# A hybrid encoder block on one Trainium2 core: two input groups without GpSimd, half of the shift made by narrow fp32 products

## The chip, the core and the metric

The kernel runs on one core of one Trainium2 chip, in one launch. The metric is the device time of that launch in microseconds (us). A core has TensorE (PE, matrix products into PSUM), VectorE (DVE), ScalarE (ACT), GpSimd (POOL), and SyncE (SP), which issues most of the loads here.

## What is computed

The reference is one layer of an encoder block with batch 1, 512 positions and 2048 channels, in fp32. Only its beginning is touched:

```python
mod = jax.nn.silu(c) @ w_ada + b_ada                 # c: (1, 2048), w_ada: (2048, 6*2048)
shift1, scale1, gate1, shift2, scale2, gate2 = jnp.split(mod, 6, axis=-1)
h = rms_norm(x, norm1_w) * (1 + scale1) + shift1
p = h @ w_in                                         # Fourier | q | k | v | o gate | i/f gates
...
x = x + gate1 * (mix @ w_out)                        # mix: Fourier and mLSTM heads
h2 = rms_norm(x, norm2_w) * (1 + scale2) + shift2
...
return rms_norm(x, norm_f_w)
```

The normalisation factor of a position (one over the root mean square of its 2048 channels) is known only when all of x has been read, and a channel of scale1 or shift1 only when 2048 weights have been multiplied with silu(c) and summed.

## The kernel before, in words

x lies transposed: sixteen tiles of 128 channels by 512 positions. An fp32 product is made of three products of a reduced type (F32R), high part by high, high by remainder, remainder by high: `kouter` (L231 to L237) issues these three for every PSUM bank of a group, for one channel tile k (a step). `split` (L113 to L122) makes the high part of a weight tile on ScalarE (L120) and the remainder on VectorE (L121). A name that ends in h or l is such a part (wh6h and wh6l of the tile wh6).

**Group 1** (L393 to L400) makes the o gate: eight banks, so 24 products of 512 columns in a step. It uses x times the scale alone (`A1`); the normalisation factor rb1 and the shift are brought in later. `scale_tile(k)` (L360 to L382) prepares step k: it loads 128 rows of w_ada as two tiles of 128x1024, multiplies each with a row of silu(c) that is repeated over the partitions (`silb`) and sums it along the row (`ada_unit`, L157 to L172). On VectorE that is one instruction (L167) that leaves the sum too; on GpSimd it is a multiply (L169), and ScalarE sums its result (L177). `ada_cols` (L179 to L189) adds the two halves and the bias in three instructions of 128x1 (L183, L186, L189), and then ScalarE casts x times the scale (L373), VectorE makes its remainder (L374), and the squares of x are summed (L380, L381). Of the two halves of a step, GpSimd takes the second, but for k = 0.

**Group 2** (L452 to L466) makes q and k of three heads: six banks, 18 products in a step, from the same x times scale. Beside it, `shift_unit(k)` (L423) makes the 128 shifts of tile k in the same way, with the second half on GpSimd for two k of three, and `shift_tile(k)` (L427 to L450) overwrites tile k by the full h: x times rb1 (on GpSimd, L433 or L435), times A1, plus the shift. It also sums the shift's own share of q and k (`qkb`, L447, L449). rb1 comes from sixteen small products (L405, and L348 in `bcast_rows`) and a copy (L461) in the course of the group. When all is made, eight tiles of the o gate are multiplied by rb1 on GpSimd (L477 to L479, after GpSimd's last multiply of weights), and the products of v begin (L341 to L343), which read the overwritten tiles.

A scheduler sets the order of the instructions on each engine when the kernel is built; each engine then runs its own list in that order. Loads are issued by SP in one list too: a load whose buffer is still in use holds up those behind it. The w_ada tiles of 128x1024 rotate through eight buffers (`ar`, L208), other weights through four (`raw`).

Of the kernel before, what the change touches and what calls it, by code (L numbers as in the profile page):

```python
# [10 lines left out]
F32 = mybir.dt.float32  # L11
F32R = mybir.dt.float32r
I32 = mybir.dt.int32
AF = mybir.ActivationFunctionType
ALU = mybir.AluOpType
PSUM = bass.MemoryType.PSUM

P = 128
D = 2048
S = 512  # L20
KT = D // P
# [27 lines left out]


@with_exitstack
def block_kernel(ctx: ExitStack, tc: tile.TileContext, xT, vec, wada, wg, wqk, wv0, wvu,
                 wout, wup, wdown, cst, rmask, ftab, crow, cvec, outT):
    nc = tc.nc
    mm = nc.tensor.matmul
# [32 lines left out]
    onesf = const.tile([P, P], F32, name="onesf")  # L88
# [57 lines left out]
    ada = {"late": []}  # L146
# [11 lines left out]
    def ada_unit(mod, slot, k, u, w, sb, pool=None):  # L158

        if "ring" in ada:  # L160
            r = ada["ring"][k % 4]
        else:
            r = ada["p"].tile([P, w], F32, tag="ar", bufs=ada["n"], name=f"ad{mod}_{k}_{u}")
        nc.sync.dma_start(r, wada[mod, k, :, u * w:(u + 1) * w])
        part = adaD[:, slot, k, u:u + 1]
        if not ((k if w == S else u) % 2 if pool is None else pool):
            nc.vector.scalar_tensor_tensor(r, r, 1.0, sb, op0=ALU.mult, op1=ALU.mult, accum_out=part)  # L167
        else:
            ada["pool"] = nc.gpsimd.tensor_tensor(r, r, sb, op=ALU.mult)  # L169
            ada["late"].append((r, part))  # L170
            if w == S:
                ada_late(1 if "ring" in ada else 2)  # L172
# [32 lines left out]
    pst = pa.enter_context(ExitStack())  # L205
    pS = pst.enter_context(tc.tile_pool(name="pS", bufs=1))
    silb = pS.tile([P, D], F32, tag="silb", name="silb")
    ada.update(p=pS, n=8)  # L208
    o_t = [None] * 8

    def evac_o(ps, i):
# [148 lines left out]
    def scale_tile(k):  # L360
        ak = A1[:, k:k + 1]
        for u in (range(2) if k else (1, 0)):
            ada_unit(1, 0, k, u, 1024, silb[:, u * 1024:(u + 1) * 1024], pool=u and k)
        if k == 0:
            load_x(0)
            load_consts()
        r = raw_tile(wg[k, :, 0:1024], 1024, f"wg{k}")
        if k + 1 < KT:
            load_x(k + 1)
        ada_cols(ak, "n1", 1, 0, k, 1, 2)  # L370
        t = x_t[k]
        bt[k], btl[k] = big_tiles(k)
        nc.scalar.activation(bt[k], t, AF.Copy, scale=ak)  # L373
        nc.vector.scalar_tensor_tensor(btl[k], t, ak, bt[k].bitcast(F32), op0=ALU.mult, op1=ALU.subtract)  # L374
        w = split(r, 1024, f"wg{k}")
        if k == 0:
            nc.scalar.activation(ssq1, t, AF.Square)
        else:
            sq = T512("sq")
            nc.scalar.activation(sq, t, AF.Square)  # L380
            nc.vector.tensor_tensor(ssq1, ssq1, sq, op=ALU.add)  # L381
        return w  # L382
# [36 lines left out]
    def g2_weights(k):  # L419
        r = raw_tile(wg[k, :, 1024:1792], 768, f"wh{k}")  # L420
        return r, split(r[:, :768], 768, f"wh{k}")

    def shift_unit(k):  # L423
        for u in range(2):
            ada_unit(0, 0, k, u, 1024, silb[:, u * 1024:(u + 1) * 1024], pool=u and k % 3 < 2)

    def shift_tile(k, r):  # L427

        sk = S1[:, k:k + 1]
        t = T512("ht")  # L430
        raw = 0 < k < 13
        if raw:
            nc.gpsimd.tensor_tensor(t, x_t[k], rb1, op=ALU.mult)  # L433
        else:
            nc.gpsimd.tensor_tensor(t, bt[k].bitcast(F32), btl[k].bitcast(F32), op=ALU.add)  # L435
            nc.vector.tensor_tensor(t, t, rb1, op=ALU.mult)
        ada_cols(sk, "g", 0, 0, k, 1, 2)
        bt[k], btl[k] = big_tiles(k)
        if raw:
            nc.scalar.activation(t, t, AF.Identity, scale=A1[:, k:k + 1], bias=sk)  # L440
            nc.scalar.activation(bt[k], t, AF.Copy)
            nc.vector.tensor_tensor(btl[k], t, bt[k].bitcast(F32), op=ALU.subtract)
        else:
            nc.scalar.activation(bt[k], t, AF.Identity, bias=sk)
            nc.vector.scalar_tensor_tensor(btl[k], t, sk, bt[k].bitcast(F32), op0=ALU.add, op1=ALU.subtract)
        if k == 0:
            nc.vector.tensor_scalar(qkb, r[:, 0:256], sk, None, op0=ALU.mult)  # L447
        else:
            nc.vector.scalar_tensor_tensor(qkb, r[:, 0:256], sk, qkb, op0=ALU.mult, op1=ALU.add)  # L449
# [23 lines left out]
    for i, x in enumerate((7, 6, 2, 3, 4, 5)):  # L473
        r = pX.tile([P, S], F32, tag=f"x{x}", name=f"qkraw{i}")
        nc.vector.tensor_tensor(r, g_ps[i], rb1, op=ALU.mult)
        raws.append(r)
    with tc.issue_after(ada["pool"].ins):  # L477
        for i in range(8):
            nc.gpsimd.tensor_tensor(o_t[i], o_t[i], rb1, op=ALU.mult)  # L479
    v0_first = [v0_unit(u) for u in range(2)]  # L480
    pst.close()
    pA = pa.enter_context(tc.tile_pool(name="pA", bufs=1))
# [950 lines left out]
def _pack(inp):  # L1433
# [10 lines left out]
                            cols(f("norm_f_w")), np.tile(f("b_gates")[gsort], 8)[:, None], cols(f("mlstm_norm_w")), cols(f("c")[0])], 1))  # L1444
    cvec = C(np.stack([cols(wc[0]), cols(wc[1]), cols(wc[2]), cols(f("b_conv"))], 1))
    wada = C(f("w_ada").T).reshape(6, KT, P, D)
    wi = f("w_in")
    q0, k0, v0, o0, g0 = 1024, 1536, 2048, 3072, 4096
    t = lambda a, n=P: np.arange(a, a + n)
# [14 lines left out]
    for nk in KBLOCKS:  # L1464
# [4 lines left out]
    parts.append(wd[f0:].transpose(1, 2, 0, 3).reshape(P, KT * NPLAIN * P))  # L1469
    wdown = C(np.concatenate(parts, 1))  # L1470
    cst, rm = _consts()
    return {"xT": xT, "vec": vec, "wada": wada, "wg": wg, "wqk": wqk, "wv0": wv0, "wvu": wvu,
            "wout": wout, "wup": wup, "wdown": wdown, "cst": cst, "rmask": rm, "ftab": _tables(),
            "crow": C(f("c")), "cvec": cvec}

# [15 lines left out]
```

## Time and profile before

| | us |
|---|---|
| runs shown: lowest, median, highest of 3 | 2191.17, 2195.56, 2200.74 |
| the profiled execution | 2191.24 |
| its span in the trace | 2189.5 |
| PE busy | 2042.6 (93%) |
| DVE busy | 1810.1 (83%) |
| ACT busy | 1129.5 (52%) |
| POOL busy | 507.6 (23%) |

The trace has each engine's instructions with start, duration, and, where the engine was idle before one, what ended that wait. A matmul's duration overlaps with the next one's; the distance between two starts is its price in a row of them. "PEclk" is the granted clock of TensorE as a share of full speed. The time of the profiled execution stands 1.7 us above its span; a difference in the span is taken as one in the time.

### The profile page before, as it was taken

Reading aid. Unit: us, or ns where it says so; the run is one execution under the profiler, and the core shown is the slowest. Engines: PE = TensorE matmul, PEld = TensorE weight load, DVE = VectorE, ACT = ScalarE, POOL = GpSimd, SP = SyncE. Lnnn points to the kernel's source line nnn. Section 1 sums busy time; section 2 is a strip of 40 time slices with the busy share of each in tenths; the row PEclk is TensorE's granted clock in tenths of the full one; section 3 lists DMA queues with packets and bytes.
Section 4 is the critical chain, followed back from the end, with each engine's and each line's share of the span. In section 5 each row is a group of like instructions: output and inputs, shape, how many; then the busy total and the mean of one; then the engine's idle time right before and its main releaser. Section 6 shows DMA issues by size and latency. Waiting matters only on the chain.

```text
span 2189.5 us, 38669 instructions
## 1 busy us (share of the span) xinstructions
PE 2042.6 (93%) x15036; PEld 1946.1 (89%) x15036; DVE 1810.1 (83%) x2604; ACT 1129.5 (52%) x1749; POOL 507.6 (23%) x415
## 2 busy tenths in 40 slices
PE   6986989898999979999999999999999899999996
PEld 4764889888887969999999999999999899999996
DVE  7999897887766689989899899989887678778766
ACT  4553446554444565555555554554555455555553
POOL 3447442421434201110110111110110011111134
PEclk9998999999999989999999999999999999999998
DMA  8873864644597646666666667567566897896785
GB/s 331 289 248 113 287 216 148 193 156 150 187 324 267 185 127 185 197 184 199 184 195 197 189 192 217 160 193 221 155 188 212 317 273 183 278 262 162 196 226 155
DMA packets 165436, 456.44 MB, mean 208 GB/s; under 512 B 18354, under 2 KB 22978, under 8 KB 165252
## 3 DMA queue, kind: packets, MB, share of 16 engines
q1 hardware_dynamic: 135860, 371.64, 50.4%
q0 software_dynamic: 28304, 81.28, 17.5%
q8 instruction: 118, 1.93, 0.4%
q10 hardware_dynamic: 1088, 1.05, 0.1%
q14 instruction: 66, 0.54, 0.1%
HBM read 386.52 MB, written 67.37 MB: 207 GB/s over the span
## 4 chain that ended last, share of the span: by engine, by line
PE 56%; DVE 19%; DMA 15%; issue 5%; ACT 3%; POOL 1%; SPq 0%; POOLq 0%; DVEq 0%; ACTq 0%
DMA ad<-wada 5%; DVE ad L167 5%; DMA ring<-wada 2%; DMA gkept<-gh 2%; DMA dn_0g<-wdown 1%; PE N L628 1%; DMA mov<-gkept 1%; DMA wb<-wg 1%; PE dz L283 1%; PE dz L282 1%; PE dz L284 1%; DVE A L183 1%; PE wo L284 1%; PE wo L282 1%; PE wo L283 1%
## 5 line engine op out<-in xcount | busy, mean ns | idle before, releaser
L1332 POOL DMA_DIRECT2D xkept<-cr x80 | 69.8, 1007 | 379.7 <-DVE cr L1137 362.8
L169 POOL TENSOR_TENSOR ad<-ad,silu 128x512 f32<-128x512 f32 x60 | 96.7, 1626 | 195.2 <-DVE silu L246 152.9
L167 DVE SCALAR_TENSOR_TENSOR ad<-ad,silu 128x512 f32<-128x512 f32 x125 | 116.5, 944 | 28.5 <-DMA ad<-wada 28.2
L169 POOL TENSOR_TENSOR ad<-ad,silb 128x1024 f32<-128x1024 f32 x26 | 71.1, 2738 | 80.1 <-DMA ad<-wada 62.1
L1199 ACT ACTIVATE u<-cr,cvt 128x512 f32<-128x512 f32 x88 | 71.6, 815 | 33.1 <-DVE cr L1135 31.5
L177 ACT ACTIVATE ad<-ad 128x512 f32<-128x512 f32 (+1 forms) x86 | 64.9, 755 | 43.3 <-POOL ad L169 43.1
L1248 POOL DMA_DIRECT2D gkept<-gh x38 | 29.8, 784 | 222.3 <-ACT gh L1243 171.5
L169 POOL TENSOR_TENSOR ring<-ring,silu 128x512 f32<-128x512 f32 x36 | 52.8, 1468 | 84.1 <-DMA ring<-wada 84.1
L1201 DVE SCALAR_TENSOR_TENSOR u<-cr,cvt,u 128x511 f32<-128x511 f32 x88 | 65.5, 746 | 0.5 <-ACT u L1199 0.5
L1202 DVE SCALAR_TENSOR_TENSOR u<-cr,cvt,u 128x511 f32<-128x511 f32 x88 | 65.5, 745 | 0.0
L167 DVE SCALAR_TENSOR_TENSOR ad<-ad,silb 128x1024 f32<-128x1024 f32 x38 | 59.3, 1562 | 7.4 <-DMA ad<-wada 7.4
L177 ACT ACTIVATE ring<-ring 128x512 f32<-128x512 f32 x36 | 22.7, 631 | 61.1 <-POOL ring L169 61.0
L1243 ACT ACTIVATE gh<-gst 128x1024 fp32r<-128x1024 f32 (+1 forms) x38 | 36.0, 947 | 29.8 <-DMA gkept<-gh 24.5
L1246 DVE TENSOR_TENSOR gst<-gst,gh 128x1024 fp32r<-128x1024 f32 (+1 forms) x38 | 41.4, 1089 | 11.2 <-ACT gh L1243 11.2
L167 DVE SCALAR_TENSOR_TENSOR ring<-ring,silu 128x512 f32<-128x512 f32 x35 | 32.4, 935 | 21.1 <-DMA ring<-wada 21.1
L283 PE MATMUL dz<-mov,dz_0h 128*128 128x256 f32 (+1 forms) x156 | 48.1, 309 | 0.0
L284 PE MATMUL dz<-mov,dz_0l 128*128 128x256 f32 (+1 forms) x156 | 48.0, 308 | 0.0
L282 PE MATMUL dz<-mov,dz_0h 128*128 128x256 f32 (+1 forms) x156 | 47.9, 307 | 0.0
L628 PE MATMUL N<-v,ph 128*128 128x258 f32 x160 | 34.3, 298 | 13.9 <-DVE es L611 7.8
L507 POOL TENSOR_TENSOR sb<-sb,wb 128x512 f32<-128x512 f32 x22 | 34.5, 1569 | 44.7 <-ACT wb L506 39.8
L284 PE MATMUL wo<-mov,wo_0l 128*128 128x512 f32 x104 | 41.7, 401 | 2.8 <-DVE wo_0l L121 2.8
L284 PE MATMUL wo<-mov,wo_8l 128*128 128x512 f32 x104 | 41.7, 403 | 2.0 <-DVE wo_8l L121 2.0
(4045 smaller groups left out, 9788.0 us busy)
## 6 DMA issues: line engine op xcount, KB each, us to landing
ad<-wada SPq DMA_DIRECT2D x185, 256.0 KB, 4.1
ad<-wada SPq DMA_DIRECT2D x64, 512.0 KB, 6.4
mov<-gkept SPq DMA_DIRECT2D x52, 512.0 KB, 10.2
xkept<-cr POOLq DMA_DIRECT2D x80, 256.0 KB, 6.0
ring<-wada SPq DMA_DIRECT2D x71, 256.0 KB, 4.5
wo<-wout SPq DMA_DIRECT2D x32, 512.0 KB, 5.2
wb<-wg SPq DMA_DIRECT2D x48, 256.0 KB, 4.4
dz<-wdown SPq DMA_DIRECT2D x26, 384.0 KB, 3.5
```

The costliest lines, as they stand in the source:

```text
L167: nc.vector.scalar_tensor_tensor(r, r, 1.0, sb, op0=ALU.mult, op1=ALU.mult, accum_out=part)
L169: ada["pool"] = nc.gpsimd.tensor_tensor(r, r, sb, op=ALU.mult)
L177: nc.scalar.activation(r, r, AF.Copy, accum_out=part)
L282: mm(ps, wh[:, sl], rh[k], start=st, stop=False)
L283: mm(ps, wh[:, sl], rl[k], start=False, stop=False)
L284: mm(ps, wl[:, sl], rh[k], start=False, stop=sp)
L628: mm(np_[:, 0:258], l[:, sl], v[:, r, t, :], start=i == 0, stop=i == n - 1)
L1199: nc.scalar.activation(u, r, AF.Identity, bias=cv(3, ch), scale=cv(1, ch))
L1201: nc.vector.scalar_tensor_tensor(u[:, 1:S], r[:, 0:S - 1], cv(0, ch), u[:, 1:S], op0=ALU.mult, op1=ALU.add)
L1202: nc.vector.scalar_tensor_tensor(u[:, 0:S - 1], r[:, 1:S], cv(2, ch), u[:, 0:S - 1], op0=ALU.mult, op1=ALU.add)
L1246: nc.vector.tensor_tensor(lo, part, hi.bitcast(F32), op=ALU.subtract)
L1332: nc.gpsimd.dma_start(xkept[4 * d + 2 * j + r], rows[j][r], accum_op=ALU.add)
```

## The change

In both groups no weights and no x go to GpSimd any more. `scale_tile` puts both halves on VectorE. `shift_tile` makes x times A1 times rb1 in one instruction of VectorE. The shift of eight of the sixteen tiles (k = 2, 3, 6, 7, 10, 11, 14, 15) isn't made by `ada_unit`: `shift_pair` makes that of two tiles on TensorE, from a rearranged copy of the same weights (`wsh`). The stationary operand is 128x32, with silu(c) in its first column and zeros in the others; four products of 256 columns, each of another sixteenth of the 2048 inputs, write to four groups of 32 PSUM partitions, and four rounds of them accumulate. ScalarE copies the bank, two more products with ones add the four partial sums up, and VectorE adds the bias. The eight multiplies of the o gate stay on GpSimd, now pinned in program order instead of being held behind GpSimd's last multiply of weights. There are seven `ar` buffers instead of eight.

```diff
-    ada.update(p=pS, n=8)
+    ada.update(p=pS, n=7)
...
     def scale_tile(k):
...
-            ada_unit(1, 0, k, u, 1024, silb[:, u * 1024:(u + 1) * 1024], pool=u and k)
+            ada_unit(1, 0, k, u, 1024, silb[:, u * 1024:(u + 1) * 1024], pool=False)
...
+    c32 = pS.tile([P, KT, 32], F32, tag="c32", name="c32")
+    nc.vector.memset(c32, 0.0)
+    nc.vector.tensor_copy(c32[:, :, 0], vcols("c", 0, KT))
+
+    def shift_pair(c):
+        bank = side(f"sp{c}")
+        for q in range(4):
+            r = pS.tile([P, 1024], F32, tag="ar", bufs=ada["n"], name=f"sp{c}_{q}")
+            nc.sync.dma_start(r, wsh[c // 2, q])
+            for i in range(4):
+                mm(bank[32 * i:32 * i + 32, 0:256], c32[:, 4 * q + i, :], r[:, i * 256:(i + 1) * 256], start=q == 0,
+                   stop=q == 3)
+        parts = T512("sp")[:, 0:256]
+        nc.scalar.activation(parts, bank[:, 0:256], AF.Copy)
+        for i in range(2):
+            mm(bank[:, 256 + i:257 + i], parts[:, i * P:(i + 1) * P], onesf[:, 0:1], start=True, stop=True)
+        nc.vector.tensor_tensor(S1[:, 2 * c:2 * c + 2], bank[:, 256:258], vcols("bada", 2 * c, 2), op=ALU.add)
+
     def shift_unit(k):
+        if k // 2 % 2:
+            if k % 2 == 0:
+                shift_pair(k // 2)
+            return
         for u in range(2):
-            ada_unit(0, 0, k, u, 1024, silb[:, u * 1024:(u + 1) * 1024], pool=u and k % 3 < 2)
+            ada_unit(0, 0, k, u, 1024, silb[:, u * 1024:(u + 1) * 1024], pool=False)
 
     def shift_tile(k, r):
...
-            nc.gpsimd.tensor_tensor(t, x_t[k], rb1, op=ALU.mult)
+            nc.vector.scalar_tensor_tensor(t, x_t[k], A1[:, k:k + 1], rb1, op0=ALU.mult, op1=ALU.mult)
         else:
-            nc.gpsimd.tensor_tensor(t, bt[k].bitcast(F32), btl[k].bitcast(F32), op=ALU.add)
+            nc.vector.tensor_tensor(t, bt[k].bitcast(F32), btl[k].bitcast(F32), op=ALU.add)
             nc.vector.tensor_tensor(t, t, rb1, op=ALU.mult)
-        ada_cols(sk, "g", 0, 0, k, 1, 2)
+        if k // 2 % 2 == 0:
+            ada_cols(sk, "g", 0, 0, k, 1, 2)
         bt[k], btl[k] = big_tiles(k)
-        if raw:
-            nc.scalar.activation(t, t, AF.Identity, scale=A1[:, k:k + 1], bias=sk)
-            nc.scalar.activation(bt[k], t, AF.Copy)
-            nc.vector.tensor_tensor(btl[k], t, bt[k].bitcast(F32), op=ALU.subtract)
-        else:
-            nc.scalar.activation(bt[k], t, AF.Identity, bias=sk)
-            nc.vector.scalar_tensor_tensor(btl[k], t, sk, bt[k].bitcast(F32), op0=ALU.add, op1=ALU.subtract)
+        nc.scalar.activation(bt[k], t, AF.Identity, bias=sk)
+        nc.vector.scalar_tensor_tensor(btl[k], t, sk, bt[k].bitcast(F32), op0=ALU.add, op1=ALU.subtract)
...
-    with tc.issue_after(ada["pool"].ins):
-        for i in range(8):
-            nc.gpsimd.tensor_tensor(o_t[i], o_t[i], rb1, op=ALU.mult)
+    for i in range(8):
+        pinned(nc.gpsimd.tensor_tensor, o_t[i], o_t[i], rb1, op=ALU.mult)
...
+    wsh = C(f("w_ada")[:, 0:D].reshape(4, 4, P, 4, 2, 256)[:, :, :, :, 1].transpose(3, 0, 2, 1, 4)).reshape(4, 4, P, 1024)
```

The scheduler orders the new kernel anew. VectorE, one step of group 1, before (ad is a tile of w_ada with its tile and half, A the scale, wg a weight tile, mov the remainder of x, ssq the sum of squares):

```order
L167 SCALAR_TENSOR_TENSOR ad_11_0_618,adaD<-ad_11_0_618,silb 128x1024
L183 TENSOR_TENSOR A_83<-adaD 128x1
L186 SCALAR_TENSOR_TENSOR A_83<-A_83,vt 128x1
L189 TENSOR_TENSOR A_83<-A_83,vt 128x1
L121 TENSOR_TENSOR wg11l<-wg_624,wg11h 128x1024
L381 TENSOR_TENSOR ssq_100<-ssq_100,sq 128x512
L374 SCALAR_TENSOR_TENSOR mov<-x_532,A_83,mov 128x512
```

And now:

```order
L167 SCALAR_TENSOR_TENSOR ad_10_0_562,adaD<-ad_10_0_562,silb 128x1024
L374 SCALAR_TENSOR_TENSOR mov<-x_478,A_83,mov 128x512
L167 SCALAR_TENSOR_TENSOR ad_10_1_565,adaD<-ad_10_1_565,silb 128x1024
L183 TENSOR_TENSOR A_83<-adaD 128x1
L186 SCALAR_TENSOR_TENSOR A_83<-A_83,vt 128x1
L121 TENSOR_TENSOR wg11l<-wg_614,wg11h 128x1024
L189 TENSOR_TENSOR A_83<-A_83,vt 128x1
L381 TENSOR_TENSOR ssq_100<-ssq_100,sq 128x512
```

Both halves of w_ada stand in the step, and a remainder of weights between the second and the third of the small instructions.

VectorE in group 2, the last instructions ahead of the remainder of the seventh weight tile, wh6l, before (S is the shift, rb the copied normalisation factor, ht x times it):

```order
L461 COPY rb_903<-rps 128x512
L167 SCALAR_TENSOR_TENSOR ad_7_0_1232,adaD<-ad_7_0_1232,silb 128x1024
L436 TENSOR_TENSOR ht<-ht,rb_903 128x512
L183 TENSOR_TENSOR S_84<-adaD 128x1
L186 SCALAR_TENSOR_TENSOR S_84<-S_84,vt 128x1
L449 SCALAR_TENSOR_TENSOR qkb<-wh_1122,S_84,qkb 128x256
L445 SCALAR_TENSOR_TENSOR mov<-ht,S_84,mov 128x512
L167 SCALAR_TENSOR_TENSOR ad_8_0_1271,adaD<-ad_8_0_1271,silb 128x1024
L121 TENSOR_TENSOR wh6l<-wh_1122,wh6h 128x768
```

And now, from the first pair's shift on and with a piece left out (sp is a pair's bank):

```order
L440 TENSOR_TENSOR S_84<-sp_1024,vt 128x2
L167 SCALAR_TENSOR_TENSOR ad_9_0_1311,adaD<-ad_9_0_1311,silb 128x1024
L183 TENSOR_TENSOR S_84<-adaD 128x1
L468 SCALAR_TENSOR_TENSOR qkb<-wh_955,S_84,qkb 128x256
...
L186 SCALAR_TENSOR_TENSOR S_84<-S_84,vt 128x1
L456 SCALAR_TENSOR_TENSOR ht<-x_340,A_83,rb_891 128x512
L456 SCALAR_TENSOR_TENSOR ht<-x_386,A_83,rb_891 128x512
L456 SCALAR_TENSOR_TENSOR ht<-x_432,A_83,rb_891 128x512
L456 SCALAR_TENSOR_TENSOR ht<-x_478,A_83,rb_891 128x512
L121 TENSOR_TENSOR wh6l<-wh_1118,wh6h 128x768
```

In the piece left out stand another L167, four L464 (as L445 before), two L468, an L183 and an L186. The copy of rb1 (L480) is 28 instructions ahead of wh6l now, where it was eight ahead.

TensorE at the same place, before, where step 6 follows step 5:

```order
L237 MATMUL h_895<-mov,wh5l 128x512
L237 MATMUL h_896<-mov,wh5l 128x512
...
L235 MATMUL h_891<-mov,wh6h 128x512
L236 MATMUL h_891<-mov,wh6h 128x512
L235 MATMUL h_892<-mov,wh6h 128x512
```

And now:

```order
L237 MATMUL h_881<-mov,wh5l 128x512
L434 MATMUL sp_1186<-sp_0_1187,c_882 32x256 x4
L434 MATMUL sp_1186<-sp_1_1193,c_882 32x256 x4
L434 MATMUL sp_1186<-sp_2_1199,c_882 32x256 x4
L434 MATMUL sp_1186<-sp_3_1205,c_882 32x256 x4
L434 MATMUL sp_1348<-sp_0_1349,c_882 32x256 x4
L434 MATMUL sp_1348<-sp_1_1355,c_882 32x256 x4
L235 MATMUL h_876<-mov,wh6h 128x512
```

The second pair and half of the third stand between the two steps. The first pair stands within step 3, the third's other half within step 6, the fourth pair within and between steps 8 and 9. On GpSimd, the first work in the list is now the eight multiplies of the o gate, which need rb1.

## Rows read from the trace of the kernel before

**Rows 1.** Busy time by stretch: length, PE, PEld, DVE, ACT, POOL (instructions), PEclk, DMA share, GB/s

```profile
13.00:124.00 111.00, 96.80 (x385) 75.33 (x386) 104.79 (x135) 56.09 (x90) 49.72 (x19) 0.97 0.87 309
124.00:228.50 104.50, 77.15 (x308) 60.64 (x307) 102.30 (x135) 40.28 (x64) 65.39 (x32) 0.87 0.51 167
228.50:400.00 171.50, 157.70 (x1128) 148.98 (x1128) 145.93 (x248) 92.97 (x174) 74.40 (x47) 0.97 0.68 223
```

**Rows 2.** Products by weight tile: duration ns least/median/most, first and last start us

```profile
L235 PE MATMUL g<-mov,wg0h x8: 397/628/796, 13.3 to 19.2; 128*128 128x512 f32 x8
...
L237 PE MATMUL g<-mov,wg0l x8: 387/391/398, 19.7 to 21.3; 128*128 128x512 f32 x8
...
L235 PE MATMUL g<-mov,wg4h x8: 389/391/500, 51.3 to 53.0; 128*128 128x512 f32 x8
...
L235 PE MATMUL g<-mov,wg5h x8: 389/389/389, 56.9 to 58.5; 128*128 128x512 f32 x8
...
L237 PE MATMUL g<-mov,wg5l x8: 388/389/389, 58.9 to 62.1; 128*128 128x512 f32 x8
...
L235 PE MATMUL h<-mov,wh0h x6: 387/389/486, 123.8 to 128.6; 128*128 128x512 f32 x6
```

**Rows 3.** Timeline of a later step of group 1: start us, duration us, engine, instruction

```profile
76.92 1.21 DVE L167 SCALAR_TENSOR_TENSOR ad<-ad,silb 128x1024 f32<-128x1024 f32 x1
77.71 2.67 POOL L169 TENSOR_TENSOR ad<-ad,silb 128x1024 f32<-128x1024 f32 x1 [3.06 <-DMA ad<-wada]
...
78.06 2.34 DVE L183 TENSOR_TENSOR A<-adaD 128x1 f32<-128x1 f32 x1
80.43 0.16 DVE L186 SCALAR_TENSOR_TENSOR A<-A,vt 128x1 f32<-128x1 f32 x1
...
80.74 1.23 DVE L121 TENSOR_TENSOR wg10l<-wg,wg10h 128x1024 fp32r<-128x1024 f32 x1
...
81.88 0.68 DVE L381 TENSOR_TENSOR ssq<-ssq,sq 128x512 f32<-128x512 f32 x1
...
82.48 0.74 DVE L374 SCALAR_TENSOR_TENSOR mov<-x,A,mov 128x512 fp32r<-128x512 f32 x1
...
83.14 1.22 DVE L167 SCALAR_TENSOR_TENSOR ad<-ad,silb 128x1024 f32<-128x1024 f32 x1
```

**Rows 4.** Timeline of the first four steps, GpSimd and VectorE

```profile
15.44 3.02 POOL L169 TENSOR_TENSOR ad<-ad,silb 128x1024 f32<-128x1024 f32 x1 [15.00 <-DMA ad<-wada]
...
24.73 2.62 DVE L374 SCALAR_TENSOR_TENSOR mov<-x,A,mov 128x512 fp32r<-128x512 f32 x1 [0.79 <-ACT mov L373]
...
28.99 3.48 POOL L169 TENSOR_TENSOR ad<-ad,silb 128x1024 f32<-128x1024 f32 x1 [2.19 <-DMA ad<-wada]
```

**Rows 5.** Instructions by line and shape, 117 to 232 us: busy us, mean ns

```profile
L167 DVE SCALAR_TENSOR_TENSOR ad<-ad,silb 128x1024 f32<-128x1024 f32 x20 | 30.8, 1541 | 0.0
```

**Rows 6.** fp32 products and one weight load: timeline, tile and lines views

```profile
139.27 1.16 PE L348 MATMUL rps<-dg,onesf 128*128 128x128 f32 x8 [0.84 <-DVE dg L142]
...
L155 PE MATMUL cb<-cr,onesf x4: 1056/1056/1185, 2.2 to 4.9; 1*128 1x512 f32 x4
...
L518 PEld LDWEIGHTS sbp<-onesf,sb 128*128 128x128 f32 x24 | 3.7, 239 | 0.0
```

**Rows 7.** Timeline at the end of group 2, GpSimd and VectorE

```profile
203.14 14.16 POOL L479 TENSOR_TENSOR o<-o,rb 128x512 f32<-128x512 f32 x8
...
214.14 2.03 DVE L121 TENSOR_TENSOR wh13l<-wh,wh13h 128x768 fp32r<-128x768 f32 x1
...
217.84 0.47 DVE L449 SCALAR_TENSOR_TENSOR qkb<-wh,S,qkb 128x256 f32<-128x256 f32 x1
218.23 0.95 DVE L121 TENSOR_TENSOR wh14l<-wh,wh14h 128x768 fp32r<-128x768 f32 x1
```

**Rows 8.** Timeline of group 2 where wh6l was late, TensorE

```profile
159.26 0.79 PE L237 MATMUL h<-mov,wh6l 128*128 128x512 f32 x1 [6.79 <-DVE wh6l L121]
...
159.85 0.63 PE L235 MATMUL h<-mov,wh6h 128*128 128x512 f32 x1
```

More of the change, by code (lines that the diff above doesn't have):

```diff
@@ L51, in block_kernel @@
 @with_exitstack
-def block_kernel(ctx: ExitStack, tc: tile.TileContext, xT, vec, wada, wg, wqk, wv0, wvu,
+def block_kernel(ctx: ExitStack, tc: tile.TileContext, xT, vec, wada, wsh, wg, wqk, wv0, wvu,
                  wout, wup, wdown, cst, rmask, ftab, crow, cvec, outT):
@@ L1471, in _pack @@
     cst, rm = _consts()
-    return {"xT": xT, "vec": vec, "wada": wada, "wg": wg, "wqk": wqk, "wv0": wv0, "wvu": wvu,
+    return {"xT": xT, "vec": vec, "wada": wada, "wsh": wsh, "wg": wg, "wqk": wqk, "wv0": wv0, "wvu": wvu,
             "wout": wout, "wup": wup, "wdown": wdown, "cst": cst, "rmask": rm, "ftab": _tables(),
```

## The prediction

> **What bounds the kernel now.** I read the busy time by stretch first [rows 1]. In the first group of products (13 to 124 us, sixteen steps of 24 products into eight PSUM banks) and in the second (124 to 228.5 us, sixteen steps of 18) VectorE is busy for 104.8 of 111 and 102.3 of 104.5 us, TensorE for 96.8 and 77.2, and TensorE's granted clock in the second is 0.87 on average, between its two levels of 1.2 and 2.4 GHz. So VectorE sets the pace of both. In the remainder up to 400 us TensorE is the busier engine; nothing of that is edited, apart from eight GpSimd multiplies that come earlier.
>
> Then the starts of the products, by weight tile [rows 2]. Within a step they follow one another every 0.226 us (24 starts from 56.9 to 62.1 us), so a step can't take less than 5.43 us. From the fifth step's start, 51.3 us, to the end of the group at 123.8 us (where the second begins) twelve steps take 72.5 us: 65.2 us of products and 7.3 us lost. The first four take 13.3 to 51.3 us; the first, much of it at the clock's lower level (0.63 us where others take 0.39), needs 8.4 us and three more 16.3, so 13.3 us are lost there. Group 1 loses 20.6 us in all.
>
> Then VectorE's own timeline of one step [rows 3]. A 128x1 addition, the first of three small ones that turn two partial sums into the scale, takes 2.34 us, and the small ones behind it take 0.16. It begins while GpSimd's 2.67 us multiply (77.71 us) is under way and ends just as that ends. It does no more work than they do; it waits for GpSimd, and with it waits the scale, ScalarE's cast and TensorE's next step. In the early steps the same happens to large instructions: 2.62 us for the remainder of x, which takes 0.74 in the later step [rows 3, 4].
>
> **The change, group 1.** Removed: 15 GpSimd multiplies, and the ScalarE sums that read them. Added: 15 multiplies of 128x1024 on VectorE. By the distances of the starts in [rows 3], a step of VectorE is now 2 x 1.14 (multiplies) + 1.14 (weight remainder) + 0.60 + 0.66 (sum of squares, remainder of x) + 3 x 0.16 = 5.2 us, under TensorE's 5.43. VectorE has more to do and is faster, because the wait goes. Nor do the loads bound it: in the first four steps the second half of the scale's weights lands at 15.44 and 28.99 us, three steps apart, 4.5 us each [rows 4]. Of the 20.6 us I take 18 as regained, because 0.2 us a step is little margin; the ends are 10.7 (below, second rival) and 20.6. The seven load buffers instead of eight cost nothing while that margin holds: three and a half steps of 5.43 us are 19 us of cover for a load of a few us. Without the cover the load's 4.5 us would show in every step.
>
> **The change, group 2.** The GpSimd multiplies of x by rb1 and of weights go, and twelve VectorE subtractions are replaced by as many of another form; VectorE gets twelve products of three factors (0.74 us, the form of the x remainder in [rows 3]). Half of the shift's 32 multiplies leave VectorE: of 21 there 16 stay, whose mean was 1.54 us where an undisturbed one takes 1.21 [rows 3, 5]. What now ends the group is a chain over three engines. I count from the group's start.
>
> - Steps 0 to 2 and 11 products of step 3 are 65 x 0.226 = 14.7 us; two sets of eight small products at 1.16 us each [rows 6] and a copy, taken at the 0.7 us of the 128x512 addition in [rows 3], make rb1 at 17.7.
> - TensorE then does the first pair's 16 products, C us, 21 ordinary ones (4.8) and 0.3 of small ones: the first pair's shift is there at 22 + C.
> - VectorE's order, shown above, has 18 instructions between that shift and wh6l: five small (0.8), two multiplies (2.4), three of qkb (1.4), eight of 0.74 (5.9) and wh6l itself (0.95), 11.5 us [rows 3, 7].
> - The eight GpSimd multiplies of o start as soon as rb1 exists and last 14.2 us, to 31.9. There VectorE goes at about half pace: wh13l took 2.03 us inside them, wh14l 0.95 after them [rows 7]. That part is moved, and not saved.
>
> C has no row; no product here uses 32 columns. The nearest is an fp32 product of 128 columns: two instructions, eight of them in 1.16 us [rows 6], 0.126 us from start to start (the last runs on for 0.28). With 256 columns that is at most 0.25 us each, and 32 instructions are 8.1 us a pair, one after another. Four side by side would make 2.0. I take 4, nearer to side by side because the four write disjoint PSUM partitions. The Trainium skill ("TensorE: Matmul & The Clock Gate", Part 3) gives 2.38 times for three column tiles; as an estimate by that page C would be 3.4, and the sum 1 us lower. No run here shows it.
>
> With C = 4: the shift at 26, then 5.9 us at half pace and 8.5 us at full, so wh6l at 40.4 (TensorE would be there at 27 + 2.5C = 37). Then 1.4 for the remaining products of step 6, 2 for the half pair between them, 0.3 and 2.6 us for the third pair's shift and wh7l; 162 products of steps 7 to 15 (36.6), the last pair (4.3): 87.6 us. Two stalls drop the clock, as at 159.85 us, where products take 0.63 us, after a 6.8 us wait for wh6l [rows 8]; I add 2.4. So 90 us, not 104.5: 14.5 saved. With C = 2 it is 84 to 86; with C = 8.1 TensorE's own work bounds it, 71 + 4C = 103.5, and 1 us is saved.
>
> What follows shifts as a whole, since its first products need only the split weights and the first shifted tiles, which are ready steps before.
>
> **Sum.** 18 + 14.5 = 32.5 us off the profiled execution's 2191.24: 2158.7. The median of the runs shown lies 4.3 above that execution, so 2163 against 2195.56. Half a per cent, 11 us, is about what a measurement of this kernel can tell from no change.
>
> **Rivals.**
> - *The four column groups don't overlap* (C = 8.1). For it: every product in the trace uses the whole array and is followed by the next at its own length. Against: the partitions are disjoint. Only group 1 gains, and 1 us: 2195.56 - 19 = 2177. Chance 0.16.
> - *Group 1 stays VectorE-bound.* VectorE still waits 0.79 us for ScalarE in an early step [rows 4]; in every step that makes 5.2 + 0.8 = 6.0 us, today's 72.5/12. Group 1 gains 10.7: 2170. Against: in a later step ([rows 3]) nothing waits. 0.08.
> - *The gain is given back later*: from 228.5 us VectorE has 145.9 of 171.5 us [rows 1], and a wait for a load there that doesn't move would eat the gain. Against: the loads there begin only when the second group's buffers are free. 2192. 0.05.
> - *Weight loads show.* An fp32 load takes 0.24 us [rows 6]; if none of 128 is hidden, group 2 takes 103.5 + 128 x 0.2 = 129 us, and 24.5 - 18 = 6.5 are lost: 2202. 0.05. The Trainium skill (the same page, Part 3) has a rule for this: weights are loaded beside running products only where the row group differs, and here all four use the same rows. The trace has no such case.
> - *Slower: the products run at the low clock, one by one.* Place: TensorE between steps 5 and 6 and after, where it has waited for tiles that the load queue could only fetch once earlier products freed their buffers. Price: 1.056 us for an instruction of 512 columns at the low level [rows 6], 0.53 for 256, 128 of them 68 us, so group 2 takes 71 + 68 = 139: 34.5 - 18 = 16.5 lost, 2212. It decides from 0.40 us an instruction on, where 128 of them eat both gains (51 us). 0.04.
>
> **How the numbers follow.** The forecast has 0.62, with its own range from 2152 to 2174 (C from 2 to 6, group 1 from 14 to 20.6). Faster by over 0.5% (below 2184.6): 0.62 + 0.16 + 0.08 = 0.86. Within: 0.05 + 0.05 = 0.10. Slower: 0.04. The range for 8 in 10 reaches from 2150 (both gains at their upper ends, 41 us, and the 4 us between runs) to 2184, which takes in the first two rivals.
>
> **What would show it.** Group 1: VectorE's small additions all near 0.16 us, step starts 5.4 us apart, its end near 105 us. If steps stay 6 us apart with VectorE busy throughout, the first step of the argument is wrong. Group 2: its end near 195 us; a visible wait of TensorE for wh6l, with VectorE stretched only for the 14 us of the o multiplies; the products in fours with starts closer than 0.2 us. Starts 0.25 us apart mean the first rival. If both ends move by 30 us and the time doesn't, the loss lies behind 230 us.

## The result and the profile after

The changed kernel takes **2165.99 us** (median of 4 runs, 2156.98 to 2171.10) against 2197.09 for the kernel before on the same chip: ratio 0.9857, 95% interval 0.9816 to 0.9897. It is faster by 1.4%, and both ends of the interval lie beyond the half per cent that a measurement can tell. The profiled execution took 2156.98 us, 34.3 us less than the profiled one of before; its span is 2155.1.

The busy time by stretch, cut where the groups now end, answers to [rows 1]:

```profile
13.00:106.00 93.00, 90.20 (x384) 73.25 (x385) 85.97 (x170) 38.94 (x54) 0.00 (x0) 1.00 0.99 376
106.00:197.00 91.00, 81.47 (x452) 62.37 (x451) 70.43 (x122) 25.69 (x39) 14.12 (x8) 0.94 0.52 182
```

VectorE fell from 104.8 to 86.0 us in group 1, although it makes fifteen more sums there, and from 102.3 to 70.4 in group 2. TensorE is now the busier engine in both, 90.2 of 93 and 81.5 of 91. Products by weight tile (as [rows 2]):

```profile
L235 PE MATMUL g<-mov,wg4h x8: 389/393/501, 38.1 to 39.9; 128*128 128x512 f32 x8
L235 PE MATMUL g<-mov,wg5h x8: 389/389/389, 43.7 to 45.3; 128*128 128x512 f32 x8
L235 PE MATMUL h<-mov,wh0h x6: 389/396/486, 106.1 to 111.2; 128*128 128x512 f32 x6
L237 PE MATMUL h<-mov,wh15l x6: 389/391/397, 193.2 to 196.6; 128*128 128x512 f32 x6
```

The fifth step starts at 38.1 instead of 51.3, the second group at 106.1 instead of 123.8: 17.7 us saved. Group 2 ends when the next products start, at 196.8; before, those started at 228.6. So it takes 90.7 us where it took 104.8, and the two groups together save 31.8.

VectorE's timeline of a later step of group 1 (as [rows 3]):

```profile
60.59 0.16 DVE L183 TENSOR_TENSOR A<-adaD 128x1 f32<-128x1 f32 x1
60.79 0.16 DVE L186 SCALAR_TENSOR_TENSOR A<-A,vt 128x1 f32<-128x1 f32 x1
61.15 1.22 DVE L121 TENSOR_TENSOR wg10l<-wg,wg10h 128x1024 fp32r<-128x1024 f32 x1 [0.20 <-DMA x<-xT]
...
62.96 1.22 DVE L167 SCALAR_TENSOR_TENSOR ad<-ad,silb 128x1024 f32<-128x1024 f32 x1
```

The first small addition now takes 0.16 us, where it took 2.34. In group 2, GpSimd and VectorE from rb1 (called the row rstd in the expectations below) to the weight tile of step 6, then TensorE and the loads that SP issues:

```profile
123.77 14.12 POOL L348 TENSOR_TENSOR o<-o,rb 128x512 f32<-128x512 f32 x8 [123.33 <-DVE rb L480]
```

```profile
122.93 0.69 DVE L480 COPY rb<-rps 128x512 f32<-128x512 f32 x1 [1.78 <-PE rps L348]
123.66 0.69 DVE L459 TENSOR_TENSOR ht<-ht,rb 128x512 f32<-128x512 f32 x1
124.26 6.87 DVE L456 SCALAR_TENSOR_TENSOR ht<-x,A,rb 128x512 f32<-128x512 f32 x4
131.06 3.48 DVE L464 SCALAR_TENSOR_TENSOR mov<-ht,S,mov 128x512 fp32r<-128x512 f32 x2
134.46 2.31 DVE L167 SCALAR_TENSOR_TENSOR ad<-ad,silb 128x1024 f32<-128x1024 f32 x1
...
139.50 0.15 DVE L440 TENSOR_TENSOR S<-sp,vt 128x2 f32<-128x2 f32 x1
...
145.98 2.72 DVE L456 SCALAR_TENSOR_TENSOR ht<-x,A,rb 128x512 f32<-128x512 f32 x4
148.63 0.94 DVE L121 TENSOR_TENSOR wh6l<-wh,wh6h 128x768 fp32r<-128x768 f32 x1
```

```profile
122.82 1.93 PE L434 MATMUL sp<-sp,c 128*32 128x256 f32 x32
...
129.59 0.50 PE L439 MATMUL sp<-onesf,sp 128*128 128x1 f32 x4
...
135.17 1.93 PE L434 MATMUL sp<-sp,c 128*32 128x256 f32 x32
143.34 1.08 PE L434 MATMUL sp<-sp,c 128*32 128x256 f32 x8 [6.24 <-DMA sp<-wsh]
145.66 1.08 PE L434 MATMUL sp<-sp,c 128*32 128x256 f32 x8 [1.23 <-DMA sp<-wsh]
147.60 0.80 PE L235 MATMUL h<-mov,wh6h 128*128 128x512 f32 x1 [0.86 <-ACT wh6h L120]
148.19 0.63 PE L236 MATMUL h<-mov,wh6h 128*128 128x512 f32 x1
...
153.32 1.66 PE L237 MATMUL h<-mov,wh6l 128*128 128x512 f32 x6
```

```profile
139.61 1.54 SPq L432 DMA_DIRECT2D sp<-wsh  x2
```

Four things are to be seen. The sixteen products of a pair (32 instructions) take 1.93 us. Four multiplies of x take 6.87 us while GpSimd multiplies o, and four others 2.72 after it. TensorE has the first pair's sums done at 130.1, but VectorE adds the shift only at 139.50, behind work that stands ahead of it in its order. And what TensorE then waits for are loads: those of the third pair are issued from 139.61 us on, when VectorE's sums free their buffers, and it waits 6.24 and 1.23 us for them. It doesn't wait for wh6l, which is made by 149.57 and first read at 153.32. Between 137.1 and 147.6 TensorE does little, and the granted clock is at its lower level for the first products after that (0.63 us each).

### The profile page after: what moved, and what is told of

It reads as the page before. It is cut to its first block, busy times and chain, and to the rows that moved or that the text cites. A ratio compares the mean times of both kernels' runs of the same rounds, so it can differ in the third digit from the quotient of the medians.

```text
span 2155.1 us, 38846 instructions
## 1 busy us (share of the span) xinstructions
PE 2033.8 (94%) x15180; PEld 1937.4 (90%) x15180; DVE 1756.5 (82%) x2630; ACT 1098.7 (51%) x1689; POOL 410.5 (19%) x373
## 4 chain that ended last, share of the span: by engine, by line
PE 60%; DMA 16%; DVE 14%; issue 4%; ACT 4%; POOL 1%; SPq 0%; DVEq 0%; POOLq 0%; ACTq 0%
DMA ad<-wada 6%; DVE ad L167 3%; DMA ring<-wada 2%; DMA gkept<-gh 1%; PE N L646 1%; PE h L235 1%; PE g L236 1%; PE g L237 1%; PE g L235 1%; PE h L236 1%; PE h L237 1%; DMA dn_0g<-wdown 1%; DMA dn_1d<-wdown 1%; PE un L319 1%; PE un L320 1%
## 5 line engine op out<-in xcount | busy, mean ns | idle before, releaser
L167 DVE SCALAR_TENSOR_TENSOR ad<-ad,silu 128x512 f32<-128x512 f32 x125 | 115.3, 934 | 23.9 <-DMA ad<-wada 23.1
L167 DVE SCALAR_TENSOR_TENSOR ad<-ad,silb 128x1024 f32<-128x1024 f32 x48 | 59.5, 1241 | 6.9 <-DMA ad<-wada 6.9
L177 ACT ACTIVATE ad<-ad 128x512 f32<-128x512 f32 x60 | 37.6, 628 | 40.1 <-POOL ad L169 39.7
L167 DVE SCALAR_TENSOR_TENSOR ring<-ring,silu 128x512 f32<-128x512 f32 x35 | 31.6, 915 | 21.5 <-DMA ring<-wada 21.5
L282 PE MATMUL wo<-mov,wo_8h 128*128 128x512 f32 x104 | 40.8, 395 | 0.4 <-ACT wo_8h L120 0.4
## 6 DMA issues: line engine op xcount, KB each, us to landing
mov<-gkept SPq DMA_DIRECT2D x52, 512.0 KB, 10.1
```

Of the source, the lines that this page charges most:

```text
L177: nc.scalar.activation(r, r, AF.Copy, accum_out=part)
L282: mm(ps, wh[:, sl], rh[k], start=st, stop=False)
```

## The experiments

The theory: GpSimd's multiplies, by their use of SBUF, hold VectorE's instructions that work in SBUF, those with two operands above all, and the change gains by taking GpSimd away. Its rivals: the gain is in what waited for GpSimd's results, or in the products on TensorE. Instructions are ordered by a scheduler, so edits that remove instructions change the order of others too; where that matters it is said. "Group 1" and "group 2" below are from the first product of the first group, at 13 us, and from that of the second, to the first product of what follows. A mixed tile is one that `shift_tile` has overwritten.

**The first group alone** (kernel before, one word changed):

```
-            ada_unit(1, 0, k, u, 1024, silb[...], pool=u and k)
+            ada_unit(1, 0, k, u, 1024, silb[...], pool=False)
```

> The kernel before, with only the first group's scale sums taken from GpSimd (no products on TensorE, no other edit; still eight sum buffers). Theory (GpSimd's multiplies hold VectorE, and the group is bound by VectorE): the first group ends at 105 to 107 us instead of 123.8, as in the changed kernel; the second group still takes 104 to 106 us; the run is about 18 us shorter than before, ratio 0.992. Rival A (the first group's gain is only there together with the rest, because the second group's loads and GpSimd work wait earlier): group 2 takes 110 us or more, ratio 0.995 to 1.000.

Measured: ratio 0.9913 (0.9882 to 0.9943), 2171.46 us. Group 1 ends at 103.3, group 2 takes 104.6. The theory holds, rival A falls: the first half of the gain needs nothing of the second. Group 1 even ends 2.8 us earlier than in the changed kernel.

**GpSimd multiplying for nobody** (changed kernel, `n=6`):

```
+    dum = pS.tile([P, 1024], F32, tag="dum", name="dum")
         if k:
+            pinned(nc.gpsimd.tensor_tensor, dum, silb[:, 0:1024], silb[:, 1024:2048], op=ALU.mult)
```

> The changed kernel, with fifteen GpSimd multiplies of 128x1024 put back into the first group that read only the silu row and write a tile of their own that nobody reads (one sum buffer fewer, six, to make room). Nothing waits for them. Theory (GpSimd's two reads by themselves hold VectorE's two-operand instructions): VectorE's L167 takes up to 2.4 us beside one, steps of the first group go from 5.45 to 6.5 us or more, and the run is 15 to 30 us longer than the changed kernel, ratio to before 0.992 to 1.000. Rival (the first group's gain came from what waited for GpSimd's products, ScalarE's sums of them and the adds behind those): steps stay at 5.4 to 5.6 us and the time within 3 us of the changed kernel, ratio 0.986.

Measured: 2196.31 us, ratio 1.0020 (1.0001 to 1.0040): the whole gain is gone. The steps did not stretch evenly, because nothing held the multiplies back; GpSimd did all fifteen in one run:

```profile
7.84 43.80 POOL L348 TENSOR_TENSOR dum<-silb 128x1024 f32<-128x1024 f32 x15 [7.39 <-ACT silb L156]
```

```profile
14.47 2.35 DVE L86 CAST identr<-ident 128x128 fp32r<-128x128 f32 x1
...
28.19 3.38 DVE L167 SCALAR_TENSOR_TENSOR ad<-ad,silb 128x1024 f32<-128x1024 f32 x1
...
34.89 2.17 DVE L183 TENSOR_TENSOR A<-adaD 128x1 f32<-128x1 f32 x1
37.10 0.16 DVE L186 SCALAR_TENSOR_TENSOR A<-A,vt 128x1 f32<-128x1 f32 x1
```

VectorE's sums take up to 3.38 us instead of 1.22, and the 128x1 addition takes 2.17 again. An instruction with one operand is held too: the cast takes 2.35 us, where it takes 0.22 in the changed kernel. The fifth step starts at 67.4 instead of 38.1, 29.3 us later; the twelve from there on take 66.5, 5.54 each, and group 1 ends at 133.9. Nobody read the product, so no dependency explains this. Nor does the sixth buffer: from its first sum to 68 us VectorE waits for no load, and for 0.8 us in all. The theory is shown for the stretch in which GpSimd multiplies, and outside it there was nothing to see. The multiplies also write a tile, so reads and writes are not told apart.

**The second group alone** (changed kernel, first group's sums back to `pool=u and k`).

> The changed kernel, with the first group's scale sums as before, half of them on GpSimd; the second group as changed. With the run of the first group alone it makes the two halves of the change. Theory (the two gains stand in different stretches and add): the first group ends at 122 to 126 us, the second takes 89 to 92 us, ratio to before 0.993 to 0.995. Rival (part of what the second group gained is work that the shorter first group had done for it earlier): group 2 takes 95 us or more, ratio 0.997 or more.

Measured: 2192.77 us, ratio 1.0000 (0.9980 to 1.0021). Group 2 takes 90.2 us, as the theory has it, so its gain does not depend on group 1; the ratio that the theory gave did not come. Group 1 ends at 131.7, not 122 to 126, 7.9 us later than before, which is about half of the 14.6 us. It differs from before's in the seven buffers and in the order that the scheduler made with them; the two were not tried apart. Group 2 still ends 6.8 us ahead of before's. That is lost in the stage between the products of v and the output projection, which no edit touches: it takes 299.2 us instead of 291.5, at a mean granted clock of 0.95 instead of 0.97. Why was not tried.

**Without the products** (changed kernel; all sixteen tiles of the shift summed on VectorE):

```
     def shift_unit(k):
-        if k // 2 % 2:
-            if k % 2 == 0:
-                shift_pair(k // 2)
-            return
...
-        if k // 2 % 2 == 0:
+        if True:
             ada_cols(sk, "g", 0, 0, k, 1, 2)
```

> The changed kernel, without the products on TensorE: all sixteen tiles of the shift are summed on VectorE, GpSimd still takes no part in either group's sums, seven sum buffers. VectorE gets sixteen more sums of 1.22 us and their adds, some 22 us. Theory (the products are needed: without them VectorE bounds the second group again): VectorE's 70 us of the second group become 90 to 93, the group takes 95 to 101 us, the run is 5 to 10 us longer than the changed kernel, ratio to before 0.988 to 0.991. Rival (the second group's gain came from GpSimd's absence alone): group 2 takes 90 to 92 us, ratio 0.986.

Measured: 2155.26 us, ratio 0.9820 (0.9794 to 0.9846), not slower than the changed kernel. Both expectations missed: group 2 takes 82.7 us.

```profile
106.20:188.80 82.60, 73.33 (x305) 59.15 (x304) 82.21 (x156) 23.96 (x33) 14.44 (x8) 0.92 0.53 187
```

VectorE is busy throughout, but TensorE is busy 8 us less, and step 6 starts at 131.7 instead of 147.6: the order now puts rb1 later (135 us), so that some of the shift's sums and the weight tiles of steps 6 to 8 come before GpSimd's multiplies of o. The products are not what shortened group 2.

**o's multiplies held**, called o late below (changed kernel; they read a copy of rb1 made by ScalarE after the tenth mixed tile):

```
+        if k == 9:
+            rb2[0] = pX.tile([P, S], F32, tag="x1", name="rb2")
+            with tc.issue_after(a.ins):
+                nc.scalar.activation(rb2[0], rb1, AF.Copy)
...
-        pinned(nc.gpsimd.tensor_tensor, o_t[i], o_t[i], rb1, op=ALU.mult)
+        pinned(nc.gpsimd.tensor_tensor, o_t[i], o_t[i], rb2[0], op=ALU.mult)
```

> The changed kernel, with the eight multiplies of o by the row rstd on GpSimd held until the tenth mixed tile is done (they read a copy of the row that ScalarE makes only then). Theory (those 14 us of GpSimd reads slow VectorE by some 6 us ahead of the first pair's shift, and the weight tiles of steps 6 and on wait for that shift): the first x_t multiplies take 1.7 us for two instead of 3.4, the first pair's shift is added some 5 to 7 us earlier (near 133 instead of 139.5), wh6l is ready near 143, the second group takes 84 to 86 us instead of 90.7, and the run is 5 to 6 us shorter than the changed kernel, ratio to before 0.983. Rival (wh6 waits for the loads of the third pair and for the TensorE queue, whatever VectorE does): group 2 takes 90 to 91 us, no change against the changed kernel.

Measured: 2154.73 us, ratio 0.9831 (0.9803 to 0.9859). Group 2 takes 84.5 us, 6 us less:

```profile
124.34 2.73 DVE L456 SCALAR_TENSOR_TENSOR ht<-x,A,rb 128x512 f32<-128x512 f32 x4
127.00 1.41 DVE L468 SCALAR_TENSOR_TENSOR mov<-ht,S,mov 128x512 fp32r<-128x512 f32 x2
...
132.30 0.15 DVE L440 TENSOR_TENSOR S<-sp,vt 128x2 f32<-128x2 f32 x1
...
141.43 0.95 DVE L121 TENSOR_TENSOR wh6l<-wh,wh6h 128x768 fp32r<-128x768 f32 x1
```

The shift is added 7.2 us earlier and wh6l comes 7.2 earlier. Up to the shift the order on VectorE is the same as in the changed kernel, so 7.2 us is what the 14 us of GpSimd cost there. In the time of the whole run the 6 us are not shown: the two ratios, 0.9831 and 0.9857, lie within each other's intervals.

**The shift ahead in VectorE's order** (changed kernel; the sums of tiles 8 to 11 issue after the first pair's add).

> The changed kernel, with the VectorE sums of the shift's tiles 8 to 11 put behind the first pair's shift add in VectorE's order (in the changed kernel the add stands behind both sums of tile 8, though TensorE has finished the pair's products long before). GpSimd's multiplies of o stay where they are. Theory (the weight tile of step 6 waits for the raw tile of step 2, which is only free after the first pair's shift, and the shift stands behind VectorE's queue): the shift add starts 2.5 to 5 us before 139.5, wh6l follows by as much, the second group takes 86 to 88 us instead of 90.7. Rival (the third pair's products need the sum buffers that tile 8 frees, so TensorE waits as long for their loads): group 2 takes 90 us or more, no gain.

Measured: 2164.31 us, ratio 0.9856 (0.9829 to 0.9882). The shift is added at 136.18, 3.3 us earlier, but group 2 takes 92.2 us. The rival is right: the third pair's loads leave only from 139.66 to 143.2 us, behind the sums that free their buffers; the first of them lands at 145.48, and TensorE waits 8.49 us for that pair (6.24 in the changed kernel). Nor does wh6l follow the shift: it starts at 148.47, 0.16 us earlier, since the sums that were put behind the shift still stand ahead of it. Two chains end at the same place, and shortening one by lengthening the other brings nothing.

**One column group** (changed kernel; all products of a pair into partitions 0 to 31, and the copy and the sums behind them over 32 rows):

```
-                mm(bank[32 * i:32 * i + 32, 0:256], c32[...], r[...], start=q == 0, stop=q == 3)
+                mm(bank[0:32, 0:256], c32[...], r[...], start=q + i == 0, stop=q + i == 6)
...
```

> The changed kernel, with all sixteen products of a pair put into the first column group, one sum of 32 rows, where they can't run beside each other (the same 64 products of 128x32 by 128x256, the sums then over 32 rows). Theory (four column groups run side by side, which is why the sixteen products took 1.93 us and not the 8 that the prediction's rival gave): a pair takes 7 to 8 us, four times as long; the second group takes 8 to 23 us more than 90.7, as the products stand on TensorE's path or in its stall. Rival (the products were short by themselves): a pair still takes about 2 us and the time does not change.

Measured: 2183.51 us, ratio 0.9957 (0.9935 to 0.9979).

```profile
123.14 7.09 PE L434 MATMUL sp<-sp,c 128*32 128x256 f32 x32
```

The first pair takes 7.09 us instead of 1.93, 3.7 times as long, and group 2 takes 102.9, of which TensorE works 100. Four column groups do run side by side.

**The eighth buffer back, and o late** (the tile of silu(c) moved to one that stands unused until later):

```
-    ada.update(p=pS, n=7)
+    ada.update(p=pS, n=8)
-    c32 = pS.tile([P, KT, 32], F32, tag="c32", name="c32")
+    c32 = sbp.tile([P, S], F32, tag="sb", name="c32").rearrange("p (k c) -> p k c", c=32)
```

> The run with o's multiplies held late, with the eighth sum buffer given back: the column of silu(c) with its zeros goes to a tile that stands unused in both groups, so that eight buffers of 4 KB fit. Theory (with seven buffers VectorE waits for loads in steps 3 and 8 to 12 of the first group, and the loads of the third pair come late): the first group ends at 103 to 104 us instead of 106.2, as in the run with the first group's part alone, the second takes 82 to 85 us, the run is 2 to 5 us shorter than with o late alone, ratio to before 0.980 to 0.982. Rival (TensorE's 80 us of work and its clock bound both groups by now): no change against o late alone, 0.983.

Measured: 2152.43 us, ratio 0.9798 (0.9772 to 0.9824), the lowest ratio of the study.

```profile
13.00:102.80 89.80, 89.68 (x384) 74.03 (x385) 84.31 (x167) 38.10 (x55) 0.00 (x0) 1.00 1.01 392
102.80:182.90 80.10, 79.56 (x448) 60.65 (x446) 70.28 (x120) 25.86 (x39) 13.72 (x8) 1.00 0.58 199
...
207.70:508.50 300.80, 271.41 (x1963) 259.12 (x1962) 242.21 (x502) 153.98 (x326) 106.92 (x68) 0.95 0.54 184
```

TensorE is busy for all but 0.7 us of both groups. The groups save 13.7 us against the changed kernel. The two profiled executions differ by 3.9 us only, but that of the changed kernel lies 9.0 us below its median and this one 0.7 above; by the ratios (0.9857 and 0.9798) it is some 13 us. The stage up to the output projection, in the last row, shows how executions can differ where nothing was edited; the same stage of the changed kernel, and of the run after this one:

```profile
221.30:515.70 294.40, 264.20 (x1963) 251.54 (x1962) 238.99 (x502) 152.26 (x325) 106.73 (x66) 0.98 0.56 183
...
212.00:514.80 302.80, 272.52 (x1961) 260.85 (x1961) 244.68 (x500) 153.62 (x326) 106.08 (x68) 0.94 0.54 183
```

The same 1963 products are busy for 7.2 us longer than in the changed kernel, at a granted clock of 0.95 on average instead of 0.98. That the full groups ahead of them were the cause is not shown: with the eighth buffer alone TensorE has a gap of 3.8 us in group 2 and the stage's clock is 0.94, and with GpSimd multiplying for nobody, whose first group had a clock of 0.91, it is 0.95. Why the clock differs there was not tried.

**The eighth buffer alone** (o's multiplies where the change has them).

> The changed kernel with the eighth sum buffer given back, as in the run with eight buffers, but with o's multiplies on GpSimd left where the change has them, right after the row rstd. Theory (the late multiplies of o and the eighth buffer each bring their own part): the first group ends at 103 us; in the second the multiplies slow VectorE for 14 us from the row copy on, wh6l comes some 6 us later than the 133 of the run with both edits, and the group takes 84 to 87 us against 80.1; ratio 0.982 to 0.984. Rival (with eight buffers VectorE's sums run so far ahead that the multiplies delay nothing TensorE waits for): group 2 takes 80 to 82 us, the time is that of both edits, 0.980.

Measured: 2159.00 us, ratio 0.9827 (0.9798 to 0.9855). Group 1 ends at 103.0, group 2 takes 84.2, wh6l starts at 139.7 against 132.0 with o late. The theory holds: the buffer is worth 3.1 us in group 1, and o's multiplies still cost 4 us in group 2. (They run from 115.8 us here; the order has put rb1 earlier.)

**No products, eight buffers; then o late as well.** The run without products, with `c32` removed and `n=8`; and the same with o's multiplies held until the last or the tenth mixed tile.

> The run without products on TensorE, and without the tile that held their column, so that eight sum buffers stand again: GpSimd out of both groups' sums and mixes is then nearly all that is left of the change. Theory (the second group's gain is GpSimd's absence; the products and the buffer that they took only cost): the first group ends at 103 us, TensorE-bound, the second takes 80 to 84 us as without products and with seven buffers (82.6), ratio to before 0.979 to 0.981, 8 to 14 us shorter than the changed kernel. Rival (with the first group shorter by 3 us the sums of the shift that VectorE made ahead there fall into the second): group 2 takes 86 us or more, ratio 0.982 or more.

> The run before this one, with the eight multiplies of o on GpSimd also held until the last mixed tile of the second group. Theory (what is left of VectorE's excess in the second group is the two-operand work beside those multiplies, some 6 us): group 2 takes 75 to 79 us, near TensorE's own 73, and the multiplies then cost 0 to 6 us in the next stage; ratio 0.977 to 0.980. Rival (once the multiplies of o are out of the way the products earn their place, since VectorE bounds the group without them): group 2 takes 80 us or more, no shorter than with products, eight buffers and o late (80.1), and the time is that run's 0.980 or more.

> The same with o's multiplies held only until the tenth mixed tile, as in the run with products, so that they still fall into the second group. Theory (VectorE has little slack in the second half of the group without the products, so that the multiplies cost there what they cost earlier): group 2 takes 80 to 83 us, 3 to 6 us more than with o last. Rival (by then VectorE is ahead): within 1 us of o last.

Measured: 2154.91 us, ratio 0.9838 (0.9814 to 0.9863); 2156.13, 0.9849 (0.9825 to 0.9873); 2155.56, 0.9844 (0.9817 to 0.9871). Group 2 takes 88.5, 79.1 and 87.5 us. In the first of them the rival's number came out, but from VectorE beside o's multiplies (127 to 141 us), after which TensorE waits 5.3, 3.3 and 4.8 us for weight tiles. With o last, group 2 is as long as the theory's upper end and needs no products to be short, but the time is not the theory's: the multiplies then fall on the next stage, where TensorE waits for VectorE (1.9 us at that place in the changed kernel):

```profile
PE q L282 <- DVE gt L686: 10.5, 1, 10.5
```

With o in the tenth tile's place, where group 2 is longer than either expectation, TensorE waits 13.1 us for wh12l instead. So the price of o's multiplies moves with them, unless VectorE has slack where they run. With the products it has (70 of 80 us busy), without them it hasn't (82 of 83 in the run without products). That would be what the products are good for; against the run without products and with seven buffers (0.9820), 0.9798 is not more than the intervals can hide.

## Why the prediction was right

The forecast was 2163 us and the likeliest case came true: 2165.99. Its steps:

- **Group 1, 18 us regained:** 17.7. GpSimd's multiplies were the cause, as two runs show from both sides (the first group alone, 0.9913; GpSimd multiplying for nobody, 1.0020). The second shows more than "it waits for GpSimd" says: VectorE is held without needing the result. The small additions of 0.16 and the end near 105 are there. The steps are 5.4 us apart only at first (20.9 to 26.3); from the fifth on they are 5.67 on average (68.0 us for twelve), where with eight buffers they are 5.44 (65.3 us).
- **"The seven load buffers instead of eight cost nothing while that margin holds":** this failed. With eight, the group ends at 103.0 and all of the 20.6 us is regained; the missing buffer costs 3.1 us, about the 2.6 that I left open as "little margin" without a cause.
- **rb1 at 17.7 after the group's start:** 17.5 (123.62 less 106.1).
- **C = 4 us a pair:** mis-sized; it is 1.93, and 2.0 was the lower bound that I worked out from the fp32 products of [rows 6]. I moved away from it without a row. The one-column run measured the first rival: 7.09 us against the 8.1 bound, group 2 at 102.9 us against 103.5.
- **The shift at 22 + C, 11.5 us of VectorE behind it:** this is the step that failed. It comes at 33.4 instead of 26, though TensorE had its sums done at 24.0, which is what 22 + C gives with the measured C. I counted VectorE's instructions *behind* the shift and not those *ahead* of it: six multiplies by rb1, two remainders and two sums stand between rb1 and the shift. They are 8.6 us undisturbed (123.73 to 132.30 in the run with o late, 0.9 of it a wait for a load) and 15.8 in the changed kernel (123.66 to 139.50). From the shift to wh6l's end it is then 10.1 us, not 5.9 at half pace and the rest at full, since GpSimd is done by 137.9.
- **"A visible wait of TensorE for wh6l":** the path failed here too. TensorE doesn't wait for wh6l in the changed kernel; of its waits in group 2, 7.5 us are for the third pair's loads and 2.1 for the casts wh6h and wh7h, and ScalarE in its turn waits 5.1 us for wh6's load. VectorE's order still sets when these loads can leave, but in group 2 the sum had nothing for loads.
- **wh6l at 40.4:** 43.5 after the start. C is 2 us less than I had, the queue ahead of the shift 9.4 more, what stands behind the shift 4.3 less; from wh6l to the end 47.2 us passed where I had 49.6. So 90.7 against 90 is luck in good part: errors of both signs.
- **GpSimd's multiplies of o halve VectorE's pace:** they do more: 6.87 us for what takes 2.73.
- **Weight loads:** each of the 128 loads takes about 0.11 us, so a pair's 32 are 3.5 us one after another; they fit into 1.93. The Trainium skill's rule on this ("TensorE: Matmul & The Clock Gate", Part 3: weights load beside running products only where the row group differs) does not hold for these four column groups on the same rows, and its 2.38 times for three column tiles stands beside 3.7 for four here. That loads on the same rows are hidden could be read from [rows 1] already: 148.98 us of loads and 157.70 of products, nearly all on all 128 rows, in 171.5 us.
- **What follows moves as a whole:** 31.8 us at the group's end, 34.4 in the span, but not evenly between: the first product of the output projection comes 28.8 us earlier (515.7 instead of 544.5), and 5.6 us are gained behind it, where nothing was edited. The medians differ by 31.1.

The sum counted "half of the shift's 32 multiplies leave VectorE" as part of the way to 14.5 us (by its own count it is five, 21 less 16; the other eleven were GpSimd's). The number came true, the reason only in part: without the products group 2 is 8 us shorter than with them in the changed kernel's order. The rest of the change was enough. That this is GpSimd's absence is shown in group 2 for the multiplies of o (7.2 us of VectorE's time for 14); GpSimd's other work there, the new order and the multiply by rb1 and the scale in one instruction were not tried apart.

## What to carry to other kernels

Where a tiny VectorE instruction takes as long as a large GpSimd one beside it, count a good part of the time that GpSimd multiplies as lost to VectorE, whoever waits for the result (here 29.3 us for 43.8, and 7.2 for 14); moving GpSimd's work onto VectorE may then shorten VectorE's own busy time. When work is handed to a third engine, count on the engine that takes its result back what stands ahead of that in its order, and when its loads can leave and what its buffers take from others. Before a new path is kept, run the kernel with only the old work removed.

## What was not expected of the hardware

- Fifteen GpSimd multiplies cost 29.3 us while they ran for 43.8, with nobody waiting for their result.
- Four groups of 32 columns did 16 fp32 products in 1.93 us, 0.06 us an instruction; in one group an instruction takes 0.22.
- One stage with the same products ran at a mean granted clock from 0.94 to 0.98 in the traces of this study, and was up to 8.6 us longer in TensorE's busy time, with no edit in it and no cause found.
